# Spreading expert gates through one-hots: pairs of tokens instead of fours, the low part on one engine, evictions in another order

## The chip, the cores and the metric

The kernel is written in Bass with the Tile framework for Trainium2 and runs on one core of one chip. The metric is the device time of one execution in microseconds (us). The time before is the median of three executions. A difference below 0.2% (about 6 us) is taken as no change.

## The reference

A two-layer encoder of 512 tokens and width 1024. Each layer is attention (a global and a windowed group of heads) with a layer norm, and then a retrieval layer over 16384 experts of one neuron each:

```
for every token and each of 8 heads:
  s1, i1 = the 16 best of 128 first sub-keys;  s2, i2 = the 16 best of 128 second sub-keys
  the 16 best of the 256 sums s1 + s2 -> gates g = softmax, expert = i1 * 128 + i2
  a = gelu(u[expert] . x);   out += g * a * v[expert]
h = layer_norm(alpha * h + out)
```

So every token has 128 slots (8 heads by 16), each with a gate and two indices from 0 to 127.

## The kernel before, in words

Chunk 0 of 128 tokens (`gat`) gathers the rows of its experts. The other three chunks (`dense`, 384 tokens) are computed against all experts, in 128 blocks of 128, as plain matrix products with the gate of (expert, token) as a factor, zero nearly everywhere. That factor must first be built as a dense array `G`, laid out as [group of 32 tokens][128 first indices][128 second indices][32 tokens] and kept in DRAM. Building it is the stage of this study, the **spread** (`spread()`, once per layer). It has 48 iterations of eight tokens; four iterations make one group of 32 tokens and fill one staging tile `stg`.

The 128 slots of a token lie on the partitions. In an iteration VectorE compares the numbers 0 to 127 with the tokens' indices (L817) and gets the one-hots `o12`: `o1` of the first index and `o2` of the second, in fp16. The gates come as a sum of two fp16 parts: `a_h` is `o1` times the high part (L818, VectorE), `a_l` is `o1` times the low part. `a_l` is made half by VectorE (four tokens in one instruction, L819) and half by ScalarE (four tokens in four instructions, L821). Then TensorE multiplies for each token `o2` (stationary) by `a_h` and adds `o2` by `a_l` (L826, L827): 16 matmuls of 128x128 in an iteration, four tokens to a PSUM bank. ScalarE moves each of the two banks into `stg` (L829). When a group is full, SyncE's queue writes `stg` to `G` (L835), in two pieces.

In memory the one-hots of four tokens are interleaved: tokens are the innermost index, four fp16 values (8 bytes) wide, so a matmul on one token reads its 128 values 8 bytes apart. `o12`, `a_h` and `a_l` have two buffers each, `acc` banks in PSUM there are six, `stg` two (one in each of two pools).

Between the iterations run the first of the expert products, `acts()`: the dense tokens times one block of expert rows `ut` in full fp32 (L770, eight matmuls of 128x384, each of which the trace shows as two records) and a gelu by ScalarE (L781). One such block is asked for in every fourth iteration. After the spread come the experts (L777 to L779 and L961 to L963 on TensorE). The Tile framework orders each engine's instructions itself from the program and then each engine runs its own list in order; queue, buffers and semaphores do the rest. SyncE issues the DMAs in its own list, with a ring of four buffers (`wst`) for all large weights.

Of the kernel before, what the change touches and what calls it, by code (L numbers as in the profile page):

```python
# [45 lines left out]
def encoder_kernel(ctx: ExitStack, tc: tile.TileContext, x, ln_in_g, ln_in_b, w_in, qn_g, kn_g, sink,  # L46
# [27 lines left out]
    def bc(ap, shape):  # L74
        return ap.to_broadcast(shape)
# [6 lines left out]
    def rsqrt(src, scale, eps, n, nm):  # L82
        """y = (src * scale + eps) ** -0.5 for a [P, n] operand"""
        a = sm.tile([P, 16], F32, tag="rs_a", name=nm + "a")[:, :n]
        y = sm.tile([P, 16], F32, tag="rs_y", name=nm + "y", bufs=4)[:, :n]
        t = sm.tile([P, 16], F32, tag="rs_t", name=nm + "t")[:, :n]
        v.tensor_scalar(a, src, float(scale), float(eps), op0=MUL, op1=ADD)
        v.tensor_scalar(y.bitcast(I32), a.bitcast(I32), -0.5, 1597463007.0, op0=MUL, op1=ADD)
        for _ in range(3):
            v.scalar_tensor_tensor(t, y, -0.5, y, op0=MUL, op1=MUL)  # L90
            v.tensor_tensor(out=t, in0=t, in1=a, op=MUL)  # L91
            v.scalar_tensor_tensor(y, t, 1.5, y, op0=ADD, op1=MUL)  # L92
        return y
# [6 lines left out]
    def moments(st):  # L100
        """mean and 1 / deviation from the statistics of two halves"""
        mv = sm.tile([P, 2], F32, tag="ln_mv", name="ln_mv")
        v.bn_aggr(out=mv, in_=st.rearrange("p a b -> p (a b)"))
        return mv[:, 0:1], rsqrt(mv[:, 1:2], 1.0, LN_EPS, 1, "lnr")
# [17 lines left out]
    def transpose_rows(src, dst, nm, lo=None, gain=None, halves=(0, 1)):  # L122
        """src [P, 1024] -> dst [P, 8, P] with dst[:, k, :] = src[:, k-th 128].T"""
        for q in halves:
            qs = slice(q * 4, (q + 1) * 4)
            b = acc_bank(nm)
            for i in range(4):
                k = q * 4 + i
                pe.transpose(b[:, i * P:(i + 1) * P], src[:, k * P:(k + 1) * P], ident)
            bv = b.rearrange("p (k t) -> p k t", k=4)  # L130
            if gain is not None:
                v.tensor_tensor(out=dst[:, qs, :], in0=bv, in1=bc(gain[:, qs, None], [P, 4, P]), op=MUL)
            else:
                act.copy(dst[:, qs, :], bv)
            if lo is not None:
                v.tensor_tensor(out=lo[:, qs, :], in0=bv, in1=dst[:, qs, :].bitcast(F32), op=SUB)
# [12 lines left out]
    nc.sync.dma_start(ident, ident_c)  # L149
    iota4 = cp.tile([P, P, 4], F16, name="iota4")  # L150
    nc.sync.dma_start(iota4.rearrange("p n t -> p (n t)"), iota4_c)
    look = cp.tile([P, 3, TK, 8], F16, name="look")
# [7 lines left out]
    for l in range(L):  # L160
# [3 lines left out]

# [1 line left out]
        gq = bload(qn_g[l], HD, "gq")  # L166
# [14 lines left out]
        def norm_rope(src, n, c, dst):  # L181
            """src, dst [P, n, 64]: rms norm over 64 and rotary, gains in the tables"""
            nr = pj.tile([P, 3, 8, HD], F32, tag="nr", name="nr", bufs=1)
# [22 lines left out]
        def load_split(src, nm):  # L206
            """a [1024, 256] weight as halves of 512 rows, each an exact sum of two f32r parts"""
            w = load_w(src, nm)
# [69 lines left out]

# [1 line left out]
        pj.release()  # L280
# [5 lines left out]
        def begin(c, part):  # L286
            """queries of four heads: the two f32r parts below each other, transposed"""
            if part == 0:
# [123 lines left out]

# [1 line left out]
        Q = dr.tile([P, PH, 2, P], F32, tag="Q", name=f"Q{l}")  # L414

        def sub_keys(cs, xT):
            """the best 16 sub-keys of both query halves of all heads, in steps"""
            n = len(cs) * P
# [7 lines left out]
            def split(w, p_):  # L426
                """the weights of one query half as two f32r parts"""
                wp = w[:, :, p_ * P:(p_ + 1) * P]
# [60 lines left out]
        def top16(rows):  # L489
            """the 16 largest of each row and their places, for (values, places, row) of several rows in turn"""  # L490
            for i in range(2):
# [13 lines left out]
        def fold(t, dst):  # L505
            """sum over axis 1 of t [P, 16, J] into dst [P, J]"""
            for n in (8, 4, 2):
# [12 lines left out]
        def pair_steps(st, c, tl):  # L520
            """the 16 best pairs of each head: gates and both key indices"""
            sv, ix = st["sv"], st["ix"]
# [21 lines left out]
            v.tensor_copy(xf.rearrange("p a h k -> p (a h k)"), ix.rearrange("p a h k -> p (a h k)"))  # L544
            # differences of the first index list: i1[a] is the sum of the first a + 1 of them
            v.tensor_copy(df[:, :, 0:1], xf[:, 0, :, 0:1])
# [171 lines left out]
        def gates(c):  # L718
            """gates, as two fp16 parts, and key indices with the slots on the partitions"""
            b = acc_bank("ps_t")  # L720
# [6 lines left out]
            gh = ga.tile([P, P], F16, tag="gh", name="gh", bufs=3)  # L727
            glf = ga.tile([P, P], F32, tag="glf", name="glf", bufs=3)
            gl = ga.tile([P, P], F16, tag="gl", name="gl", bufs=3)
# [5 lines left out]
            act.copy(iT.rearrange("p o a t -> p a o t"), b[:, P:3 * P].rearrange("p (a o t) -> p a o t", a=2, t=8))  # L735
            flat[c] = gh, glf, gl, iT

# [8 lines left out]
        sp = sbuf(f"sp{l}", bufs=2, side="right")  # L746
        sp.tile([P, 4, P, 4], F16, tag="o12", name="o12")
        for tag in ("ah", "al"):
            sp.tile([P, 2, P, 4], F16, tag=tag, name=tag)
        xTd = xd.tile([P, KD, ND], F32, name="xTd")  # L750
# [9 lines left out]
        def acts():  # L760
            """gelu of the dense tokens on one block of 128 experts after another"""
            for g2 in range(NB // 2):
# [21 lines left out]

# [1 line left out]
        vts = []  # L786
# [13 lines left out]
        def spread():  # L800
            for c in dense:
                for tg in range(P // TG):
                    stg = (sp, lp)[tg % 2].tile([P, NB, TG], F32, tag="stg", name="stg", bufs=1)
                    for t8 in range(TG // 8):
                        gh, glf, gl, iT = flat[c]
                        o = tg * TG + t8 * 8
                        shp = [P, 2, P, 4]

                        def tv(ap):
                            return bc(ap[:, o:o + 8].rearrange("p (q t) -> p q t", t=4)[:, :, None, :], shp)  # L810
                        sh2 = [P, 4, P, 4]
                        o12 = sp.tile(sh2, F16, tag="o12", name="o12")
                        o1, o2 = o12[:, 0:2], o12[:, 2:4]
                        iu = iT[:, o // 8].rearrange("p a (q t) -> p (a q) t", t=4)
                        a_h = sp.tile(shp, F16, tag="ah", name="ah")
                        a_l = sp.tile(shp, F16, tag="al", name="al")
                        v.tensor_tensor(out=o12, in0=bc(iota4[:, None, :, :], sh2), in1=bc(iu[:, :, None, :], sh2), op=EQ)  # L817
                        v.tensor_tensor(out=a_h, in0=o1, in1=tv(gh), op=MUL)  # L818
                        v.tensor_tensor(out=a_l[:, 1], in0=o1[:, 1], in1=bc(gl[:, None, o + 4:o + 8], [P, P, 4]), op=MUL)  # L819
                        for t in range(4):  # L820
                            act.activation(a_l[:, 0, :, t], o1[:, 0, :, t], AF.Copy, scale=glf[:, o + t:o + t + 1])  # L821
                        for q in range(2):
                            b = acc_bank("ps_g")
                            for t in range(4):
                                bs = b[:, t * P:(t + 1) * P]
                                pe.matmul(bs, o2[:, q, :, t], a_h[:, q, :, t], start=True, stop=False)  # L826
                                pe.matmul(bs, o2[:, q, :, t], a_l[:, q, :, t], start=False, stop=True)  # L827
                            t0 = t8 * 8 + q * 4
                            act.copy(stg[:, :, t0:t0 + 4].rearrange("p n t -> p t n"),  # L829
                                     b.rearrange("p (t n) -> p t n", t=4))  # L830
                        yield
# [23 lines left out]

# [1 line left out]
        ga.release()  # L857
# [181 lines left out]
def _layout(inputs):  # L1039
# [5 lines left out]
    def blocks(w, n):  # L1045
        """[L, 1024, n*256] -> [L, n, 128, 8*256]"""
        return w.reshape(L, KD, P, n, 256).transpose(0, 3, 2, 1, 4).reshape(L, n, P, KD * 256)
# [47 lines left out]
```

## Time and profile before

| | |
|---|---|
| three executions | 3176.3, 3172.87, 3172.13 us (median 3172.87) |
| the profiled execution: time, span of its trace | 3176.3 us, 3176.1 us |
| instructions | 47802 |
| TensorE busy | 97% of the span, weight loads 88% |
| VectorE, ScalarE, GpSimd busy | 77%, 45%, 24% |
[...]

The spread takes about 155 us in each layer, from 429 to 585 us in layer 0 and from 2000 to 2156 us in layer 1. Matmul durations in the trace are modelled and overlap; the distance from one start to the next says more than the duration. A row with a count (x4) stands for several instructions in a row: its second number reaches from the first start to the last end.

### The profile page before, as it was taken

To read this page: it belongs to the slowest core of one execution; us is meant where nothing else is said; L and a number is where in the kernel's file an instruction comes from. 1 tells how busy PE (TensorE), PEld (TensorE's weight loads), DVE (VectorE), ACT (ScalarE), POOL (GpSimd) and SP (SyncE) were. 2 spreads that over 40 slices of the span, in tenths; PEclk is the share of its full clock that TensorE was granted. 3 is DMA by queue.
4 is the path that set the end of the run, shared out by engine and by line. 5 is a ranking of instruction groups with operands and counts; after the bars stand their busy time and mean duration, and the time that the engine had idled before them with its cause. 6 is when DMAs were issued, how large, how long until landed. Compare 5 with 4: busy or idle time off the path is not lost. (4 is left out here: it accounts for less than half of the span.)

```text
span 3176.1 us, 47802 instructions
## 1 busy us (share of the span) xinstructions
PE 3078.8 (97%) x17858; PEld 2793.2 (88%) x17858; DVE 2443.1 (77%) x5206; ACT 1440.9 (45%) x2778; POOL 759.3 (24%) x524
## 2 busy tenths in 40 slices
PE   6999899999999999999999999999999999999998
PEld 6989888799999999999888888888999999999997
DVE  6777976677777777777777779766687777877777
ACT  2664279643333333333337542994433333333332
POOL 0000000005444445445000000000054433544540
PEclk9999999999999999999999999999999999999999
DMA  4113655648888888888520137556488888898882
GB/s 173 41 54 130 226 203 209 225 143 321 327 307 327 315 322 319 315 322 308 202 94 14 69 143 257 193 199 229 176 329 325 318 313 317 309 327 321 305 313 100
DMA packets 262233, 749.46 MB, mean 236 GB/s; under 512 B 19952, under 2 KB 130288, under 8 KB 231792
## 3 DMA queue, kind: packets, MB, share of 16 engines
q1 hardware_dynamic: 188272, 477.94, 41.6%
q0 software_dynamic: 73728, 268.47, 23.2%
q8 instruction: 140, 2.29, 0.3%
q14 instruction: 93, 0.76, 0.1%
HBM read 691.81 MB, written 54.53 MB: 235 GB/s over the span
## 5 line engine op out<-in xcount | busy, mean ns | idle before, releaser
L918 POOL DMA_INDIRECT gt<-in_dram,idx x512 | 753.1, 1471 | 2140.8 <-DVE idx L909 1286.6
L777 PE MATMUL ps_a<-xTh,uh 128*128 128x384 f32 x1824 | 609.9, 334 | 3.7 <-ACT uh L774 3.7
L779 PE MATMUL ps_a<-xTh,ul 128*128 128x384 f32 x1824 | 611.6, 335 | 0.0
L778 PE MATMUL ps_a<-xTl,uh 128*128 128x384 f32 x1824 | 610.2, 335 | 0.0
L963 PE MATMUL ff<-vh,wl 128*128 128x512 f32 x1476 | 576.0, 390 | 0.0
L961 PE MATMUL ff<-vh,wh 128*128 128x512 f32 x1476 | 574.4, 389 | 0.0
L962 PE MATMUL ff<-vl,wh 128*128 128x512 f32 x1476 | 574.0, 389 | 0.0
L994 ACT CAST vh<-vt 128x1024 fp32r<-128x1024 f32 x246 | 258.4, 1051 | 606.6 <-PE ff L963 308.9
L995 DVE TENSOR_TENSOR vl<-vt,vh 128x1024 fp32r<-128x1024 f32 x246 | 301.0, 1224 | 200.1 <-ACT vh L994 195.9
L777 PEld LDWEIGHTS ps_a<-xTh,uh 128*128 128x128 f32 x1824 | 342.4, 188 | 14.4 <-ACT uh L774 5.6
L778 PEld LDWEIGHTS ps_a<-xTl,uh 128*128 128x128 f32 x1824 | 342.4, 188 | 10.4
L1001 ACT CAST wh<-w 128x384 fp32r<-128x384 f32 x246 | 126.3, 513 | 484.0 <-DVE w L998 480.0
L924 DVE CUSTOM_DVE_ANT_0 junk<-gt,h 128x1024 bf16<-128x1024 f32 x256 | 313.0, 1223 | 41.2 <-DMA gt<-in_dram,idx 36.6
L779 PEld LDWEIGHTS ps_a<-xTh,ul 128*128 128x128 f32 x1824 | 342.2, 188 | 0.1
L963 PEld LDWEIGHTS ff<-vh,wl 128*128 128x128 f32 x1476 | 277.0, 188 | 57.7
L935 DVE SCALAR_TENSOR_TENSOR gacc<-gt,gw,gacc 128x1024 f32<-128x1024 f32 x252 | 311.3, 1279 | 18.4 <-DMA gt<-in_dram,idx 18.3
L961 PEld LDWEIGHTS ff<-vh,wh 128*128 128x128 f32 x1476 | 276.9, 188 | 49.6 <-ACT wh L1001 0.9
L962 PEld LDWEIGHTS ff<-vl,wh 128*128 128x128 f32 x1476 | 277.0, 188 | 48.8
L775 DVE TENSOR_TENSOR ul<-ut,uh 128x1024 fp32r<-128x1024 f32 x228 | 277.7, 1218 | 29.2 <-ACT uh L774 29.2
L774 ACT CAST uh<-ut 128x1024 fp32r<-128x1024 f32 x228 | 239.8, 1052 | 117.6 <-PE ps_a L778 115.6
L1002 DVE TENSOR_TENSOR wl<-w,wh 128x384 fp32r<-128x384 f32 x246 | 137.4, 559 | 155.5 <-ACT wh L1001 155.5
L817 DVE TENSOR_TENSOR o<-iota,iT 128x2048 f16<-128x2048 f16 x96 | 117.4, 1225 | 97.1 <-ACT al L821 62.0
(260 smaller groups left out, 5248.0 us busy)
## 6 DMA issues: line engine op xcount, KB each, us to landing
ut<-in_dram SPq DMA_DIRECT2D x128, 1024.0 KB
vt<-in_dram SPq DMA_DIRECT2D x128, 1024.0 KB
w_pq<-in_dram SPq DMA_DIRECT2D x48, 1024.0 KB
gg<-G SPq DMA_DIRECT2D x62, 768.0 KB
G<-stg SPq DMA_DIRECT2D x24, 1920.0 KB
w_o<-in_dram SPq DMA_DIRECT2D x24, 1024.0 KB
w_q<-in_dram SPq DMA_DIRECT2D x8, 1024.0 KB
gt<-in_dram,idx POOLq DMA_INDIRECT x512
```

The source lines that it names most:

```text
L775: v.tensor_tensor(out=ul.rearrange(ff), in0=us, in1=uh.rearrange(ff).bitcast(F32), op=SUB)
L777: pe.matmul(b[:, :ND], uh[:, k, :], xTh[:, k, :], start=k == 0, stop=False)
L778: pe.matmul(b[:, :ND], uh[:, k, :], xTl[:, k, :], start=False, stop=False)
L779: pe.matmul(b[:, :ND], ul[:, k, :], xTh[:, k, :], start=False, stop=k == KD - 1)
L918: pool.indirect_dma_start(out=t, out_offset=None, in_=src, in_offset=bass.IndirectOffsetOnAxis(ap=idx[:, j:j + 1], axis=0))
L924: v.tensor_tensor_reduce(out=jk, in0=t, in1=h[:, c, :], op0=MUL, op1=ADD, scale=1.0, scalar=0.0, accum_out=a_[:, j:j + 1])
L935: v.scalar_tensor_tensor(acc[j % 2], t, w_[:, j:j + 1], acc[j % 2], op0=MUL, op1=ADD)
L961: pe.matmul(b, wh[:, cs], vh[:, ns], start=blk == 0, stop=False)
L962: pe.matmul(b, wh[:, cs], vl[:, ns], start=False, stop=False)
L963: pe.matmul(b, wl[:, cs], vh[:, ns], start=False, stop=blk == NB - 1)
L994: act.copy(vh, vt[:, bi, :])
L995: v.tensor_tensor(out=vl, in0=vt[:, bi, :], in1=vh.bitcast(F32), op=SUB)
```

## The change

Four edits, all in the spread. The tokens are interleaved by two instead of four, so that a matmul's 128 values lie 4 bytes apart (`iota2` is cut out of the numbers 0 to 127 that the program loads, and the loaded table now sits in a buffer of the weight ring). `a_l` is one VectorE instruction for all eight tokens; ScalarE's four instructions are gone, and the fp32 low part `glf` that they read has one buffer instead of three. The evictions walk the bank in another order: before, the four tokens' 128 values one token after the other, which reads PSUM without gaps and writes `stg` 128 bytes apart; now, for each value the four tokens, which reads PSUM 512 bytes apart and writes runs of four (16 bytes). Comments are taken out as well.

```diff
-    iota4 = cp.tile([P, P, 4], F16, name="iota4")
-    nc.sync.dma_start(iota4.rearrange("p n t -> p (n t)"), iota4_c)
+    iota4 = ws.tile([P, 2048], F32, tag="wst", name="iota4").bitcast(F16)[:, :P * 4]
+    nc.sync.dma_start(iota4, iota4_c)
+    iota2 = cp.tile([P, P, 2], F16, name="iota2")
+    v.tensor_copy(iota2, iota4.rearrange("p (n t) -> p n t", t=4)[:, :, 0:2])
...
-            glf = ga.tile([P, P], F32, tag="glf", name="glf", bufs=3)
+            glf = ga.tile([P, P], F32, tag="glf", name="glf", bufs=1)
...
-                        shp = [P, 2, P, 4]
+                        shp = [P, 4, P, 2]
 
                         def tv(ap):
-                            return bc(ap[:, o:o + 8].rearrange("p (q t) -> p q t", t=4)[:, :, None, :], shp)
-                        sh2 = [P, 4, P, 4]
+                            return bc(ap[:, o:o + 8].rearrange("p (q t) -> p q t", t=2)[:, :, None, :], shp)
+                        sh2 = [P, 8, P, 2]
...
-                        iu = iT[:, o // 8].rearrange("p a (q t) -> p (a q) t", t=4)
+                        iu = iT[:, o // 8].rearrange("p a (q t) -> p (a q) t", t=2)
...
-                        v.tensor_tensor(out=o12, in0=bc(iota4[:, None, :, :], sh2), in1=bc(iu[:, :, None, :], sh2), op=EQ)
+                        v.tensor_tensor(out=o12, in0=bc(iota2[:, None, :, :], sh2), in1=bc(iu[:, :, None, :], sh2), op=EQ)
                         v.tensor_tensor(out=a_h, in0=o1, in1=tv(gh), op=MUL)
-                        v.tensor_tensor(out=a_l[:, 1], in0=o1[:, 1], in1=bc(gl[:, None, o + 4:o + 8], [P, P, 4]), op=MUL)
-                        for t in range(4):
-                            act.activation(a_l[:, 0, :, t], o1[:, 0, :, t], AF.Copy, scale=glf[:, o + t:o + t + 1])
+                        v.tensor_tensor(out=a_l, in0=o1, in1=tv(gl), op=MUL)
                         for q in range(2):
                             b = acc_bank("ps_g")
                             for t in range(4):
                                 bs = b[:, t * P:(t + 1) * P]
-                                pe.matmul(bs, o2[:, q, :, t], a_h[:, q, :, t], start=True, stop=False)
-                                pe.matmul(bs, o2[:, q, :, t], a_l[:, q, :, t], start=False, stop=True)
+                                r, e = q * 2 + t // 2, t % 2
+                                pe.matmul(bs, o2[:, r, :, e], a_h[:, r, :, e], start=True, stop=False)
+                                pe.matmul(bs, o2[:, r, :, e], a_l[:, r, :, e], start=False, stop=True)
                             t0 = t8 * 8 + q * 4
-                            act.copy(stg[:, :, t0:t0 + 4].rearrange("p n t -> p t n"),
-                                     b.rearrange("p (t n) -> p t n", t=4))
+                            act.copy(stg[:, :, t0:t0 + 4], b.rearrange("p (t n) -> p n t", t=4))
```

The order on ScalarE in the spread of layer 0, four iterations of before (`al` is the low part, `stg` an eviction, `ge` the gelu of a block):

```order
L829 COPY stg<-ps_g 128x4x128 x4
L821 ACTIVATE al<-o_5305,glf 128x128 x4
L821 ACTIVATE al<-o_5335,glf 128x128
L781 ACTIVATE ge<-ps_a 128x384
L821 ACTIVATE al<-o_5335,glf 128x128 x3
L829 COPY stg<-ps_g 128x4x128 x4
L821 ACTIVATE al<-o_5365,glf 128x128 x4
L821 ACTIVATE al<-o_5398,glf 128x128 x4
```

and the same place of the change:

```order
L830 COPY stg<-ps_g 128x128x4 x8
L783 ACTIVATE ge<-ps_a 128x384
L830 COPY stg<-ps_g 128x128x4 x8
L783 ACTIVATE ge<-ps_a 128x384
L830 COPY stg<-ps_g 128x128x4 x8
```

Between two gelus stand eight evictions and nothing else.

TensorE in the same place, where one burst of matmuls of before ends and four matmuls of `acts()` follow in one piece, as they do behind every two iterations:

```order
L827 LDWEIGHTS o_5264
L827 MATMUL ps_g<-al,o_5264 128x128
L770 MATMUL ps_a<-xTd,ut 128x384 x4
L826 LDWEIGHTS o_5305
L826 MATMUL ps_g<-ah,o_5305 128x128
L827 LDWEIGHTS o_5305
L827 MATMUL ps_g<-al,o_5305 128x128
```

and the change, between the iterations with `o_5313` and `o_5339`:

```order
L828 MATMUL ps_g<-al,o_5313 128x128
L772 MATMUL ps_a<-xTd,ut 128x384
L827 LDWEIGHTS o_5339
L827 MATMUL ps_g<-ah,o_5339 128x128
L827 LDWEIGHTS o_5339
L827 MATMUL ps_g<-ah,o_5339 128x128
L772 MATMUL ps_a<-xTd,ut 128x384
L828 LDWEIGHTS o_5339
```

The matmuls of `acts()` now stand singly for most of the stage, one of them behind the first two products with `a_h`, in front of the first with `a_l`; per four iterations they are still eight.

SyncE at the end of the spread, before (`gg` is the first read of `G` for the experts, `vt` a load of expert rows):

```order
L795 DMA gg_5123<-G_5126 128x11x128
L835 DMA G_5126<-stg 128x256
L791 DMA vt<-in_dram 128x2x1024
L795 DMA gg_5123<-G_5126 128x128
L835 DMA G_5126<-stg 128x3840
```

and the change:

```order
L797 DMA gg_5125<-G_5128 128x11x128
L793 DMA vt<-in_dram 128x2x1024
L835 DMA G_5128<-stg 128x256
L797 DMA gg_5125<-G_5128 128x128
L835 DMA G_5128<-stg 128x3840
```

The load of `vt` has moved ahead of the small write of `G`; otherwise SyncE's list is the same, as is GpSimd's.

## Rows read from the trace of the kernel before

**Rows 1.** The page's first two parts: busy time of each engine with its share of the span and its number of instructions, and the busy share, in tenths, of TensorE (PE) and ScalarE (ACT) in 40 slices of 79 us.

```profile
PE 3078.8 (97%) x17858; PEld 2793.2 (88%) x17858; DVE 2443.1 (77%) x5206; ACT 1440.9 (45%) x2778; POOL 759.3 (24%) x524
...
PE   6999899999999999999999999999999999999998
...
ACT  2664279643333333333337542994433333333332
```

**Rows 2.** [...]

```profile
436.30:582.20 145.90, 145.90 (x920) 118.36 (x919) 99.80 (x136) 145.87 (x283) 0.00 (x0) 1.00 0.51 196
600.00:1140.00 540.00, 540.00 (x2748) 493.72 (x2747) 420.39 (x755) 202.73 (x270) 186.00 (x136) 1.00 0.79 288
2007.00:2152.00 145.00, 145.00 (x917) 118.00 (x916) 99.55 (x136) 144.97 (x282) 0.00 (x0) 1.00 0.51 196
```

**Rows 3.** Two groups of instructions by line and form in the spread of layer 0 (436.3 to 582.2 us); columns are the busy us of the group, mean ns of one, idle time of the engine before them and who ended it.

```profile
L817 DVE TENSOR_TENSOR o<-iota,iT 128x2048 f16<-128x2048 f16 x45 | 55.1, 1225 | 45.4 <-ACT al L821 31.0 <-PE ps_g L827 13.3 <-ACT stg L829 0.7
L827 PEld LDWEIGHTS <-o 128*128 128x128 f16 x369 | 42.9, 116 | 5.7 <-issue 5.0
```

**Rows 4.** TensorE in order of time, two rounds of two iterations in layer 0 (start us, duration us, what); 443.31 to 446.97 are 32 matmuls, the first, the second and the last of them shown.

```profile
443.31 0.28 PE L826 MATMUL ps_g<-ah,o 128*128 128x128 f16 x1
443.41 0.30 PE L827 MATMUL ps_g<-al,o 128*128 128x128 f16 x1
...
446.97 0.29 PE L827 MATMUL ps_g<-al,o 128*128 128x128 f16 x1
447.09 2.76 PE L770 MATMUL ps_a<-xTd,ut 128*128 128x384 f32 x8
449.68 0.28 PE L826 MATMUL ps_g<-ah,o 128*128 128x128 f16 x1
...
456.06 0.28 PE L826 MATMUL ps_g<-ah,o 128*128 128x128 f16 x1
```

**Rows 5.** ScalarE in order of time, one round of four iterations in layer 0 (start us, us from the first start to the last end, what, how many).

```profile
444.49 3.93 ACT L829 COPY stg<-ps_g 128x512 f32<-128x512 f32 x4
448.22 1.78 ACT L821 ACTIVATE al<-o,glf 128x128 f16<-128x128 f16 x5
449.74 0.59 ACT L781 ACTIVATE ge<-ps_a 128x384 f32<-128x384 f32 x1
450.22 1.18 ACT L821 ACTIVATE al<-o,glf 128x128 f16<-128x128 f16 x3
...
457.30 3.98 ACT L829 COPY stg<-ps_g 128x512 f32<-128x512 f32 x4
```

**Rows 6.** VectorE in order of time, one round of two iterations in layer 0, with its waits in brackets.

```profile
447.36 1.22 DVE L817 TENSOR_TENSOR o<-iota,iT 128x2048 f16<-128x2048 f16 x1 [0.67 <-PE ps_g L827]
448.50 0.69 DVE L818 TENSOR_TENSOR ah<-o,gh 128x1024 f16<-128x1024 f16 x1
449.10 0.42 DVE L819 TENSOR_TENSOR al<-o,gl 128x512 f16<-128x512 f16 x1
449.44 0.69 DVE L818 TENSOR_TENSOR ah<-o,gh 128x1024 f16<-128x1024 f16 x1
...
453.73 1.23 DVE L817 TENSOR_TENSOR o<-iota,iT 128x2048 f16<-128x2048 f16 x1 [0.67 <-PE ps_g L827]
```

**Rows 7.** TensorE in order of time, other matmuls, whose operands lie without gaps: 128x256 in a one-pass 4-byte type (the first and the last of 22), 24 transposes of 128 columns in a row, and 128x512 in the one-pass type (the first and the last of nine).

```profile
331.09 0.28 PE L474 MATMUL ps_pq<-xT,wql 128*128 128x256 f32 x1
...
333.61 0.28 PE L474 MATMUL ps_pq<-xT,wql 128*128 128x256 f32 x1
...
426.63 2.78 PE L129 MATMUL tr_x<-ident,h 128*128 128x128 f32 x24
...
610.12 0.39 PE L961 MATMUL ff<-vh,wh 128*128 128x512 f32 x1
...
611.93 0.39 PE L963 MATMUL ff<-vh,wl 128*128 128x512 f32 x1
```

**Rows 8.** Six ScalarE copies of a whole bank whose source and target both lie without gaps, and two VectorE operations on 4-byte elements one behind the other.

```profile
427.52 3.04 ACT L134 COPY xTd<-tr_x 128x512 f32<-128x512 f32 x6
...
596.94 1.22 DVE L775 TENSOR_TENSOR ul<-ut,uh 128x1024 fp32r<-128x1024 f32 x1 [15.42 <-ACT uh L774]
598.08 1.22 DVE L995 TENSOR_TENSOR vl<-vt,vh 128x1024 fp32r<-128x1024 f32 x1
```

**Rows 9.** SyncE's queue at the end of the spread in layer 0, and the DMA rate in 40 slices of 3.65 us from 436.3 to 582.2 us.

```profile
586.78 0.32 SPq L835 DMA_DIRECT2D G<-stg  x1
...
588.55 0.32 SPq L795 DMA_DIRECT2D gg<-G  x1
...
GB/s 0 2 4 381 335 146 171 409 0 0 373 335 155 137 442 0 0 373 294 200 173 404 2 0 373 281 213 171 404 0 4 373 314 177 171 404 7 0 356 267
```

**Rows 10.** ScalarE and VectorE where the spread of layer 0 goes over into the experts.

```profile
584.81 1.94 ACT L829 COPY stg<-ps_g 128x512 f32<-128x512 f32 x2 [0.60 <-PE ps_g L827]
...
595.48 0.49 ACT L781 ACTIVATE ge<-ps_a 128x384 f32<-128x384 f32 x1 [4.67 <-PE ps_a L770]
...
599.21 0.55 DVE L998 SCALAR_TENSOR_TENSOR w<-gg,ge 128x384 f32<-128x384 f32 x1
```

**Rows 11.** Two rows of VectorE in the first 25 us of the program.

```profile
14.15 0.20 DVE L103 BATCH_NORM_AGGREGATE ln_mv<-ln_st 128x2 f32<-128x12 f32 x1
...
21.84 2.36 DVE L215 TENSOR_TENSOR wlo<-w_k,whi 128x1024 fp32r<-128x1024 f32 x2 [3.86 <-ACT whi L214]
```

More of the change, by code (lines that the diff above doesn't have):

```diff
@@ L735, in gates @@
             act.copy(iT.rearrange("p o a t -> p a o t"), b[:, P:3 * P].rearrange("p (a o t) -> p a o t", a=2, t=8))
-            flat[c] = gh, glf, gl, iT
+            flat[c] = gh, gl, iT
         for c in order[:2]:
@@ L746, in encoder_kernel @@
         sp = sbuf(f"sp{l}", bufs=2, side="right")
-        sp.tile([P, 4, P, 4], F16, tag="o12", name="o12")
+        sp.tile([P, 8, P, 2], F16, tag="o12", name="o12")
         for tag in ("ah", "al"):
-            sp.tile([P, 2, P, 4], F16, tag=tag, name=tag)
+            sp.tile([P, 4, P, 2], F16, tag=tag, name=tag)
         xTd = xd.tile([P, KD, ND], F32, name="xTd")
@@ L804, in spread @@
                     for t8 in range(TG // 8):
-                        gh, glf, gl, iT = flat[c]
+                        gh, gl, iT = flat[c]
                         o = tg * TG + t8 * 8
-                        shp = [P, 2, P, 4]
+                        shp = [P, 4, P, 2]
                         def tv(ap):
-                            return bc(ap[:, o:o + 8].rearrange("p (q t) -> p q t", t=4)[:, :, None, :], shp)
-                        sh2 = [P, 4, P, 4]
+                            return bc(ap[:, o:o + 8].rearrange("p (q t) -> p q t", t=2)[:, :, None, :], shp)
+                        sh2 = [P, 8, P, 2]
                         o12 = sp.tile(sh2, F16, tag="o12", name="o12")
-                        o1, o2 = o12[:, 0:2], o12[:, 2:4]
-                        iu = iT[:, o // 8].rearrange("p a (q t) -> p (a q) t", t=4)
+                        o1, o2 = o12[:, 0:4], o12[:, 4:8]
+                        iu = iT[:, o // 8].rearrange("p a (q t) -> p (a q) t", t=2)
                         a_h = sp.tile(shp, F16, tag="ah", name="ah")
                         a_l = sp.tile(shp, F16, tag="al", name="al")
-                        v.tensor_tensor(out=o12, in0=bc(iota4[:, None, :, :], sh2), in1=bc(iu[:, :, None, :], sh2), op=EQ)
+                        v.tensor_tensor(out=o12, in0=bc(iota2[:, None, :, :], sh2), in1=bc(iu[:, :, None, :], sh2), op=EQ)
                         v.tensor_tensor(out=a_h, in0=o1, in1=tv(gh), op=MUL)
-                        v.tensor_tensor(out=a_l[:, 1], in0=o1[:, 1], in1=bc(gl[:, None, o + 4:o + 8], [P, P, 4]), op=MUL)
-                        for t in range(4):
-                            act.activation(a_l[:, 0, :, t], o1[:, 0, :, t], AF.Copy, scale=glf[:, o + t:o + t + 1])
+                        v.tensor_tensor(out=a_l, in0=o1, in1=tv(gl), op=MUL)
                         for q in range(2):
```

## The prediction, made before the result was known

> **What bounds the kernel now.** I read the page first, then the busy time by stretch, then each engine in order of time in the stage that the diff touches. The page says that TensorE is busy in 97% of the span, with the weakest slices at the start and end [rows 1]; ScalarE is at 45% over the whole, but has two humps that reach nine tenths, and these are the two spreads. [...] A matmul's duration is modelled, so I check TensorE by its starts: 32 products of the one-hots start 0.1187 us apart (443.41 to 446.97 in 30 steps), then eight records of `acts()` take 2.59 us (447.09 to 449.68), and the next burst starts at once; a round of two iterations lasts 6.38 us and holds no gap [rows 4]. ScalarE is as full: an eviction comes every 0.93 us (3.73 for four), a scaled copy every 0.30, a gelu costs 0.48; 8 x 0.93 + 16 x 0.303 + 0.48 = 12.8 for four iterations, which is the distance from 444.49 to 457.30 and twice TensorE's 6.38 [rows 5]. Two engines stand at the limit together. VectorE waits, 31.0 us for ScalarE and 13.3 for TensorE before the compare of these 145.9 us [rows 3, 6].
>
> So the stage gets shorter only if *both* get faster, and then by no more than the next limit allows. The experts behind it are TensorE's alone and move as a whole.
>
> **ScalarE.** The 16 scaled copies go: 4.85 us of 12.8. The eight evictions stay and change their order. Now they read without gaps and write one value per 128 bytes: 0.93 us. Six copies of the same size without gaps on either side take 3.04 us in all, 0.5 each [rows 8]. A PSUM read with gaps is not in the trace. Bounds: 0.5, if only the write side costs, and 1.87, if the reads cost twice what the writes do now. I take 0.93, the nearest row, one gap for another: 8 x 0.93 + 0.48 = 7.9 us per four iterations, 3.96 per round. ScalarE stays off the path up to 1.2 us an eviction.
>
> **VectorE.** `a_l` grows from 512 to 1024 elements per partition. Start to start, the compare costs 1.14, `a_h` 0.60, `a_l` 0.34 [rows 6]; the new `a_l` is like `a_h`, 0.60. An iteration is 2.34, a round 4.68 of 6.38. The runs of equal step shrink from four fp16 to two. No row has runs of two. Bounds: the same 2.34, or the price per element of 4-byte operands, 1.14 us for 1024 [rows 8], twice what `a_h` pays: 2.28 + 1.14 + 1.14 = 4.56. I take 2.34, since a pair is still 4 bytes in a row in all three operands.
>
> **TensorE.** Sixteen matmuls per iteration as before, reading every 4 bytes instead of every 8. This is the term that decides. One-pass matmuls of 4-byte operands without gaps start 0.120 us apart for 256 columns (331.09 to 333.61 in 21 steps) and 0.226 for 512 (610.12 to 611.93 in 8): 0.415 ns a column and 13.5 ns fixed [rows 7]. For 128 columns that gives 0.067. The one-hot products need 0.1187 for 128 columns: 51 ns more, as if each column took 0.82 ns, twice. In address per time both are alike: 4 bytes in 0.415 ns, 8 bytes in 0.82, about 10 bytes per ns. If TensorE is held by how fast it moves through memory, 4 bytes apart gives 0.067 back. Upper bound: 0.1187, if the step was never the cause. Between them lie the transposes: 128 columns without gaps and still 0.109 apart ((2.78 - 0.27) / 23) [rows 7], which speaks for a price per weight load; but they are 4-byte data in another mode, and I cannot tell whether they stream at one column per cycle. I take 0.067: it is the only value in which three rows of ordinary matmuls fit one line.
>
> [...]
>
> **The round after.** TensorE 32 x 0.067 + 2.59 = 4.73; VectorE 4.68; ScalarE 3.96. TensorE and VectorE come out equal, and with two buffers each hands over to the other: a compare starts only when the products of two iterations ago are done. I add 0.3, half of the 0.67 that VectorE now waits for TensorE in a round [rows 6], since the matmuls of `acts()` stand singly in the new order and leave shorter holes: 5.05 us. Against 6.38 that is 1.33 per round; the 48 iterations are 23.5 rounds behind the first one: 31 us a layer, 62 in both.
>
> **What I count as nothing.** DMA: 196 GB/s over 145.9 us [rows 2], in bursts with gaps at zero [rows 9]; the same bytes in 145.9 x 5.05 / 6.38 = 115 us are 248 GB/s, below the bursts' 335 to 442. A group's 2.1 MB (32 tokens x 16384 experts x 4 bytes) take some 6 us at that; its `stg` is wanted again one group (10.1 us) after, so the write hides, and even with 1 MB of `ut` ahead of it (3 us) it is just in time. The load of `vt` ahead of the last small write holds back `gg` by up to 3 us; the first use of `gg` stands at 599.21, 10.7 us behind its issue at 588.55, while TensorE finishes the last blocks of `acts()` until 595.48 [rows 9, 10]; without that cover it would cost those 3 us. The pair table costs VectorE one small copy at 14.15 us, about 0.2; VectorE idles 3.86 us before 21.84 [rows 11], so also a late table of that size hides. The table takes a ring buffer that the fourth weight load wants after the copy, which is no later than that load's issue.
>
> **Sum.** The profiled execution took 3176.3 us, 3.4 above the median; 3176.3 - 62 = 3114.3, and for the median 3172.87 - 62 = 3111.
>
> **The rivals.**
> *Weight loads bound TensorE.* For it: the transposes, and loads as long as the distance. Against it: the 13.5 ns line of the others. At 0.1187 the round stays 6.38, since ScalarE's relief is worth nothing behind a full TensorE: 3173. If the loads allow 0.109, a round gains 32 x 0.0097 = 0.31, in all 47 x 0.31 = 15: 3158. Values between 0.067 and 0.109 lie between.
> *VectorE pays the price of 4-byte operands* (other side). A round would be 9.12 instead of 6.38 and VectorE the bound: 47 x 2.74 = 129, so 3302. It decides from 3.19 us per iteration. For it: no row has runs of two, and half the price per element may hang on longer ones. Against: each operand keeps its 4-byte pairs.
> *Evictions get dearer* (other side). At 1.87 us a round of ScalarE is 4 x 1.87 + 0.24 = 7.7: 47 x 1.34 = 63, so 3236. It decides from 1.53 us. For it: every read jumps 512 bytes. Against: the jump on the write side costs only 0.93 - 0.5.
> *The change does not shorten the stage, but adds waits*: VectorE's finer handover with a TensorE as slow as now; up to 0.3 per round, 47 x 0.3 = 14: 3187.
>
> **Chances.** TensorE at about 0.067 and the rest as summed: 0.50, with its own range 3094 (4.73 a round, 47 x 1.65 = 78) to 3137 (TensorE at 0.085, 5.61 a round). TensorE between, with a gain of 7 to 36 us: 0.12. Unchanged: 0.20. VectorE the bound 0.09, evictions 0.05, added waits 0.04. Below 0.2% of the time (6 us) a measurement cannot tell the kernels apart. So faster 0.62, same 0.20, slower 0.18. The range takes the first three, 3094 to 3180.
>
> **What would show it.** Right: in the profile after, one-hot products start about 0.067 us apart and the loads no longer lie back to back; the compare stays 1.22 us and both products 0.69; ScalarE idles in the spread; the distance from one gelu to the next is 10.1 us instead of 12.8, and the experts' rows are unchanged, some 31 and 62 us earlier. Wrong: starts still 0.11 to 0.12 apart (then no gain, whatever ScalarE does); a compare of 2.2 us (VectorE); evictions above 1.5 us; or `stg` waiting for DMA. If TensorE speeds up and the stage does not follow, I have mis-sized the handover between the two buffers.

## The result and the profile after

The changed kernel takes 3097.35 us (median of four executions, 3096.31 to 3098.3), the kernel before 3172.5 (four executions beside it): ratio 0.9756, 95% interval 0.9742 to 0.977, 75 us faster. Forecast were 3111 and a gain of 62, in a range from 3094 to 3180; the time lies near its lower end.

The page of the kernel after, busy time of each engine, and two stretches of layer 0, the spread and the experts (columns, here and in [rows 2]: the stretch, its length, busy us of PE, PEld (weight loads), DVE (VectorE), ACT, POOL with their instructions, granted clock as a share of full speed, DMA share, GB/s):

```profile
PE 2999.2 (97%) x17858; PEld 2699.4 (87%) x17858; DVE 2468.8 (80%) x5207; ACT 1248.0 (40%) x2394; POOL 741.0 (24%) x524
```

```profile
436.30:540.00 103.70, 102.94 (x853) 68.96 (x850) 102.50 (x128) 50.41 (x97) 0.00 (x0) 1.00 0.65 254
560.00:1100.00 540.00, 540.00 (x2746) 493.45 (x2745) 421.21 (x755) 202.81 (x269) 182.67 (x137) 1.00 0.80 290
```

Against the first two rows of [rows 2], the spread and the experts of layer 0, the experts are as before (540 of 540 us TensorE, ScalarE 203). In the spread ScalarE has fallen from full (145.87 of 145.90 us) to half (50.41 of 103.70), and the engine without a gap is now VectorE, 102.50 of 103.70, where it had two thirds (99.80 of 145.90). TensorE still looks full, but its ends are modelled; by its starts (start us, duration, what; one iteration's products, `acts()` in between) it isn't:

```profile
481.28 0.22 PE L828 MATMUL ps_g<-al,o 128*128 128x128 f16 x1
...
482.02 0.22 PE L828 MATMUL ps_g<-al,o 128*128 128x128 f16 x1
482.08 0.86 PE L772 MATMUL ps_a<-xTd,ut 128*128 128x384 f32 x2
...
483.74 0.22 PE L828 MATMUL ps_g<-al,o 128*128 128x128 f16 x1
```

Fourteen one-hot products start from 481.28 to 482.02, 0.057 us apart, where [rows 4] had 0.1187. Then come records of `acts()`, and the next row of products begins 2.46 us after the first: 16 x 0.057 + 4 x 0.324 = 2.2 are work. VectorE shows why (in order of time, without a wait in brackets on any row):

```profile
446.69 1.21 DVE L819 TENSOR_TENSOR o<-iota,iT 128x2048 f16<-128x2048 f16 x1
447.94 0.69 DVE L820 TENSOR_TENSOR ah<-o,gh 128x1024 f16<-128x1024 f16 x1
448.55 0.68 DVE L821 TENSOR_TENSOR al<-o,gl 128x1024 f16<-128x1024 f16 x1
449.15 1.22 DVE L819 TENSOR_TENSOR o<-iota,iT 128x2048 f16<-128x2048 f16 x1
```

Compare, high part, low part, and the next compare 449.15 - 446.69 = 2.46 us behind the first: 1.25 + 0.61 + 0.60. The durations are those of [rows 6] (1.22 and 0.69), runs of two cost nothing that shows. ScalarE waits for TensorE ahead of nearly every pair of evictions, and a pair takes 1.07 us; [rows 5] had 3.93 for four. One of the pairs:

```profile
452.62 1.07 ACT L830 COPY stg<-ps_g 128x512 f32<-128x512 f32 x2 [1.34 <-PE ps_g L828]
```

TensorE's largest wait in the stretch 436.3 to 540 us (engine and line, whom it waits for, us in total, times, longest):

```profile
PEld L827 <- DVE ah L820: 12.7, 23, 1.1
```

The weight load ahead of the first product of an iteration waits for `ah`; some of the 12.7 us lie beside matmuls that still run. In [rows 6] it was VectorE that waited for TensorE.

**Where the 75 us come from.** All 14 blocks of `acts()` have to be through before the experts begin, also those behind the last eviction. So the stage is best counted as TensorE's work from its first one-hot product to the last record of `acts()`. TensorE before, in order of time: the first product, and what stands behind the last one; and all records of `acts()` there (count, ns of one, first and last start):

```profile
429.25 0.28 PE L826 MATMUL ps_g<-ah,o 128*128 128x128 f16 x1
...
585.19 10.26 PE L770 MATMUL ps_a<-xTd,ut 128*128 128x384 f32 x26
```

```profile
L770 PE MATMUL ps_a<-xTd,ut x224: 483/486/847, 431.1 to 595.0; 128*128 128x384 f32 x112
```

The kernel after, TensorE's first product and its last records of `acts()`, and the gelu of the last block:

```profile
427.83 0.22 PE L827 MATMUL ps_g<-ah,o 128*128 128x128 f16 x1 [0.16 <-ACT iT L737]
...
547.85 6.02 PE L772 MATMUL ps_a<-xTd,ut 128*128 128x384 f32 x18
```

```profile
553.90 0.49 ACT L783 ACTIVATE ge<-ps_a 128x384 f32<-128x384 f32 x1 [2.92 <-PE ps_a L772]
```

Before: 429.25 to 585.19 + 10.26 = 595.45, 166.2 us, of which 768 x 0.1187 = 91.2 are products (48 x 16 of them) and 224 x 0.324 = 72.6 `acts()` (2.59 / 8 a record, [rows 4]): 2.4 idle. After: 427.83 to 547.85 + 6.02 = 553.87, 126.0 us, 768 x 0.0573 = 44.0 (0.0573 is the mean distance in the bursts of the stage) and the same 72.6: 9.4 idle. Products give 47.2 back; 7.0 of it are lost again in waits, 1.0 of them for ScalarE's copy of `xTd` at the start of the stage, the others beside a VectorE without a gap; and the stage begins 1.4 earlier: 41.6 in layer 0, which is the distance between the gelus of the last block, 595.48 [rows 10] and 553.90. The 1.4 can't be laid to the change: in the profiles of the nine experiments below the first product stands anywhere from 426.42 to 429.37, and why is open. In layer 1 the last gelu of the stage stands 81.57 us earlier than before, 40.0 more:

```profile
2164.54 0.49 ACT L781 ACTIVATE ge<-ps_a 128x384 f32<-128x384 f32 x1 [4.67 <-PE ps_a L770]
```

```profile
2082.97 0.49 ACT L783 ACTIVATE ge<-ps_a 128x384 f32<-128x384 f32 x1 [2.92 <-PE ps_a L772]
```

These 81.6 are those of the two profiled executions; before's was 3.8 above its median, after's 1.0 below, and 1.6 lie outside the spans (3176.3 - 3176.1 against 3096.31 - 3094.5): 75.2.

### The profile page after: what moved, and what is told of

Its sections match the earlier page's. It is cut to its first block, busy times and chain, and to the rows that moved or that the text cites. A ratio compares the mean times of both kernels' runs of the same rounds, so it can differ in the third digit from the quotient of the medians.

```text
span 3094.5 us, 47374 instructions
## 1 busy us (share of the span) xinstructions
PE 2999.2 (97%) x17858; PEld 2699.4 (87%) x17858; DVE 2468.8 (80%) x5207; ACT 1248.0 (40%) x2394; POOL 741.0 (24%) x524
## 5 line engine op out<-in xcount | busy, mean ns | idle before, releaser
L918 POOL DMA_INDIRECT gt<-in_dram,idx x512 | 734.5, 1435 | 2078.8 <-DVE idx L909 1206.1
L780 PEld LDWEIGHTS ps_a<-xTl,uh 128*128 128x128 f32 x1824 | 342.4, 188 | 10.4
L772 PE MATMUL ps_a<-xTd,ut 128*128 128x384 f32 x448 | 172.7, 501 | 1.7 <-ACT xTd L134 1.7
```

The costliest lines, as they stand in the source:

```text
L780: pe.matmul(b[:, :ND], uh[:, k, :], xTl[:, k, :], start=False, stop=False)
L918: pool.indirect_dma_start(out=t, out_offset=None, in_=src, in_offset=bass.IndirectOffsetOnAxis(ap=idx[:, j:j + 1], axis=0))
```

## The experiments

The theory: TensorE's rate in the products is set by the distance of the values that it reads, TensorE and ScalarE stood at the limit together, and VectorE is the limit now. The rivals: ScalarE's relief alone made the gain; TensorE's alone did; the order of the evictions is a part of it; the distance matters through the weight loads.

**Four tokens interleaved, the rest of the change kept.**

```diff
...
-                        shp = [P, 4, P, 2]
+                        shp = [P, 2, P, 4]
...
-                        sh2 = [P, 8, P, 2]
+                        sh2 = [P, 4, P, 4]
...
```

> The whole change, but with four tokens interleaved as before (a matmul reads its 128 values 8 bytes apart): a_l all on VectorE, ScalarE with evictions in runs of four only. Theory A (the step of TensorE's operands set the 0.1187 us per product): products again 0.118 to 0.119 us apart, a round of two iterations 6.38 us, ScalarE half idle, time 3163 to 3173 (a shorter tail at most). Rival B (ScalarE's relief is the gain, the step nothing): products near 0.06 apart, time 3097 to 3130.

Measured: 3172.48 us, ratio 0.9992 (0.9983 to 1.0001). TensorE in order of time, the first and the last of twelve products, and busy time in the stage:

```profile
464.11 0.30 PE L828 MATMUL ps_g<-al,o 128*128 128x128 f16 x1
...
465.41 0.29 PE L828 MATMUL ps_g<-al,o 128*128 128x128 f16 x1
```

```profile
436.00:546.00 110.00, 110.00 (x690) 86.51 (x689) 84.41 (x101) 44.14 (x77) 0.00 (x0) 1.00 0.49 192
```

They stand (465.41 - 464.11) / 11 = 0.118 apart, ScalarE is busy 44 of 110 us, and nothing is gained. ScalarE's relief is worth nothing behind a full TensorE.

**The interleave by two alone.** ScalarE keeps half of `a_l`, the evictions their old order.

```diff
...
-                        v.tensor_tensor(out=a_l, in0=o1, in1=tv(gl), op=MUL)
+                        v.tensor_tensor(out=a_l[:, 2:], in0=o1[:, 2:], in1=tv(gl)[:, 2:], op=MUL)
+                        for t in range(4):
+                            act.activation(a_l[:, t // 2, :, t % 2], o1[:, t // 2, :, t % 2], AF.Copy, scale=glf[:, o + t:o + t + 1])
...
-                            act.copy(stg[:, :, t0:t0 + 4], b.rearrange("p (t n) -> p n t", t=4))
+                            act.copy(stg[:, :, t0:t0 + 4].rearrange("p n t -> p t n"),
+                                     b.rearrange("p (t n) -> p t n", t=4))
```

> The interleave by two alone: half of a_l stays with ScalarE (four scaled copies per iteration), evictions in the order of before. Theory A (two engines stood at the limit together): products about 0.057 apart in their bursts, but ScalarE full with 8 x 0.93 + 16 x 0.30 + 0.48 = 12.7 us per four iterations, so the spread keeps its length: 3165 to 3175. Rival B (TensorE alone was the bound, ScalarE only followed it): 3100 to 3130.

Measured: 3162.64 us, ratio 0.9962 (0.9948 to 0.9975). Busy time in the stage, and ScalarE in order of time:

```profile
436.00:546.00 110.00, 98.45 (x713) 63.84 (x712) 78.97 (x110) 109.99 (x228) 0.00 (x0) 1.00 0.53 206
```

```profile
447.42 0.49 ACT L783 ACTIVATE ge<-ps_a 128x384 f32<-128x384 f32 x1
...
452.19 2.51 ACT L823 ACTIVATE al<-o,glf 128x128 f16<-128x128 f16 x8
454.52 3.79 ACT L832 COPY stg<-ps_g 128x512 f32<-128x512 f32 x4
...
459.50 0.53 ACT L783 ACTIVATE ge<-ps_a 128x384 f32<-128x384 f32 x1
```

ScalarE is busy 109.99 of 110 us and sets the pace; the products of a burst stand 0.057 apart, and gelu to gelu is 12.1 us where [rows 5] had 12.8. So both limits were real, but the time lies just outside what I expected: eight scaled copies take 2.51 us here (2.67 to 2.75 before) and four evictions 3.79 (3.93 to 4.02). That the evictions, which are the same instructions, get 4% shorter was not expected; they do so in the next experiment too (3.82), where VectorE makes all of `a_l`. The cause stays open.

**The change with the old evictions** (the second hunk above alone).

> The change with the evictions of before (PSUM read without gaps, writes 128 bytes apart). Theory A (VectorE with 2.46 us per iteration is the bound now): evictions 0.93 instead of 0.49, ScalarE 8 x 0.93 + 0.48 = 7.9 us per four iterations against VectorE's 9.8, so the time stays: 3096 to 3100, perhaps one to two us more at the ends of the stage. Rival B (the new order of the evictions is a part of the gain): 3105 to 3120.

Measured: 3098.76 us, ratio 0.9761 (0.9747 to 0.9774), against 0.9756 of the change. ScalarE is busy 91.39 of 110 us and still not the limit; VectorE has the same 108.70 as in the change:

```profile
436.00:546.00 110.00, 108.42 (x894) 72.78 (x893) 108.70 (x136) 91.39 (x103) 0.00 (x0) 1.00 0.67 259
```

With `a_l` on VectorE the order of the evictions is worth nothing that shows.

**Eight tokens interleaved** (`shp = [P, 1, P, 8]`).

> The change with eight tokens interleaved (a matmul reads its 128 values 16 bytes apart). Theory A (TensorE's operands come at a rate of addresses, about 10 bytes per ns, once the step is wide enough): products 0.21 to 0.23 apart, a round 32 x 0.22 + 2.6 = 9.6 us instead of 6.4, 47 rounds x 3.2 = 150 us above the kernel before: 3300 to 3350. Rival B (a step over some limit costs one fixed factor of two, whatever its size): 0.118 apart, 3165 to 3175.

Measured, one execution: 3439.28 us. TensorE, the first and the last of 32 products, eight records of `acts()`, and the last records of the stage; then stretches with the granted clock in the third column from the end:

```profile
436.91 0.40 PE L828 MATMUL ps_g<-ah,o 128*128 128x128 f16 x1
...
444.14 0.41 PE L829 MATMUL ps_g<-al,o 128*128 128x128 f16 x1
...
456.38 4.89 PE L773 MATMUL ps_a<-xTd,ut 128*128 128x384 f32 x8
...
719.92 7.68 PE L773 MATMUL ps_a<-xTd,ut 128*128 128x384 f32 x18
```

```profile
436.00:440.00 4.00, 4.00 (x18) 2.42 (x17) 0.96 (x1) 1.07 (x2) 0.00 (x0) 1.00 0.00 0
440.00:444.00 4.00, 4.00 (x19) 2.50 (x18) 1.22 (x1) 1.17 (x2) 0.00 (x0) 0.53 0.00 0
456.00:460.00 4.00, 4.00 (x9) 2.26 (x8) 3.40 (x5) 0.58 (x1) 0.00 (x0) 0.50 0.79 334
436.00:546.00 110.00, 110.00 (x367) 63.77 (x366) 45.08 (x55) 23.55 (x41) 0.00 (x0) 0.69 0.24 96
```

7.23 / 31 = 0.233 us: 0.057, 0.118 and 0.233 for 4, 8 and 16 bytes. The distance doubles with the step, and rival B falls; the time lies outside both ranges. The products alone cost 2 x 768 x (0.233 - 0.1187) = 176 us; the time is 264 above the kernel before. The rest is the clock, which no theory had moving. It stands at 1.00 where the stage of before runs, and here, with products 0.233 apart and no gap between TensorE's starts, at 0.69 in the mean of 110 us, and anywhere from 0.50 to 1.00 in stretches of 4 us. The products don't notice (the burst spans a stretch at 1.00 and one at 0.53, 18 and 19 records in 4 us), but the `acts()` between them do: at 0.50 eight records take 4.89 us, where [rows 4] had 2.76. The stage of layer 0 runs from its first product at 426.42 to 719.92 + 7.68 = 727.60, 301.2 us; 768 x 0.233 = 178.9 are products, and the 122.3 left are 49.7 more than the 72.6 of `acts()` before. With the 2.4 us that were idle before and a start 2.8 us earlier taken off, that is 44.5 in this layer; twice that, an estimate for layer 1, is 89 against the missing 88. The experts play next to no part: from 900 to 1500 us the clock is back at 1.00 (0.95 from 700 to 900 us, where the stage ends).

**Which operand.** The compare in two halves, with the stationary `o2` by fours and the moving `a_h`, `a_l` by twos, and the reverse.

```diff
+    iota4 = cp.tile([P, P, 4], F16, name="iota4")
...
-                        o1, o2 = o12[:, 0:4], o12[:, 4:8]
...
+                        o1 = o12[:, :8 * P].rearrange("p (q n t) -> p q n t", q=4, t=2)
+                        o2 = o12[:, 8 * P:].rearrange("p (q n t) -> p q n t", q=2, t=4)
...
-                        v.tensor_tensor(out=o12, in0=bc(iota2[:, None, :, :], sh2), in1=bc(iu[:, :, None, :], sh2), op=EQ)
+                        v.tensor_tensor(out=o1, in0=bc(iota2[:, None, :, :], [P, 4, P, 2]), in1=bc(iT[:, o // 8, 0].rearrange("p (q t) -> p q t", t=2)[:, :, None, :], [P, 4, P, 2]), op=EQ)
+                        v.tensor_tensor(out=o2, in0=bc(iota4[:, None, :, :], [P, 2, P, 4]), in1=bc(iT[:, o // 8, 1].rearrange("p (q t) -> p q t", t=4)[:, :, None, :], [P, 2, P, 4]), op=EQ)
...
```

> The change, but the stationary operand o2 interleaved by four tokens (its load reads 8 bytes apart), the moving operands a_h and a_l by two (4 bytes apart); the compare becomes two of half the size. Theory A (the step slows the moving stream only, and loads hide behind it): products 0.057 apart, the time that of the change plus at most 0.05 us per iteration for the split compare, 3097 to 3105. Theory B (each operand for itself is held by its bytes, and the longer of load and stream sets the distance): 0.118 apart, 3165 to 3175. Theory C (load and stream share one rate): 0.088 apart, a round of two iterations 32 x 0.088 + 2.6 = 5.4 us, 3115 to 3130.

> The reverse: the moving operands a_h and a_l interleaved by four (8 bytes apart), the stationary o2 by two (4 bytes apart); the compare in two halves. Theory A (moving stream only) and theory B (the longer of the two): products 0.118 apart, 3165 to 3175. Theory C (shared rate): 0.088 apart, 3115 to 3130. A fourth, D (only the load of the stationary operand is slowed): 0.057 here and 0.118 in the other one.

Measured: stationary by fours 3097.38 us, ratio 0.9752 (0.9737 to 0.9767), the same as the change; moving by fours 3169.34, ratio 0.998 (0.997 to 0.9989), nearly the kernel before. Of the first, sixteen products (the first and the last) and the weight loads (count, busy us, mean ns); of the second, thirteen products and the weight loads:

```profile
463.58 0.22 PE L828 MATMUL ps_g<-ah,o 128*128 128x128 f16 x1
...
464.48 0.22 PE L829 MATMUL ps_g<-al,o 128*128 128x128 f16 x1
```

```profile
L828 PEld LDWEIGHTS <-o 128*128 128x128 f16 x342 | 37.5, 114 | 20.5 <-DVE ah L820 10.4 <-issue 7.1
```

```profile
463.83 0.30 PE L828 MATMUL ps_g<-ah,o 128*128 128x128 f16 x1
...
465.23 0.30 PE L829 MATMUL ps_g<-al,o 128*128 128x128 f16 x1
```

```profile
L829 PEld LDWEIGHTS <-o 128*128 128x128 f16 x261 | 29.7, 114 | 5.0 <-issue 2.5
```

0.90 / 15 = 0.060 and 1.40 / 12 = 0.117. The moving stream is what is slowed. Theory A holds, B, C and D fall. The loads take 114 ns instead of 97 in the change, and hide: one starts every 0.060. But they take 114 in the second run too, where the stationary operand is only 4 bytes apart, so the length of a load's record does not tell which operand is wide. VectorE's four halves take 0.60 each here, 2.41 an iteration, a little less than 2.46; the time doesn't follow, since 22 records of `acts()` stand behind the last product instead of 18.

**No interleave** (each operand contiguous for a token).

```diff
...
-                        shp = [P, 4, P, 2]
+                        shp = [P, 8, P, 1]
...
-                        sh2 = [P, 8, P, 2]
+                        sh2 = [P, 16, P, 1]
...
```

> The change with no interleave at all: each token's 128 values lie without gaps (2 bytes apart), and the tokens' indices and gates are repeated 128 times for VectorE. Theory A (0.057 is what TensorE needs for 128 columns, the step of 4 bytes costs nothing any more): products 0.055 to 0.058 apart in their bursts; theory B (still held by bytes): 0.03 to 0.05. For VectorE, theory C (it keeps its rate only while each operand brings two fp16 in a row): compare 2.3 and products of the gates 1.15 to 1.2, an iteration about 4.6, 3097 + 96 x 2.1 = 3300; theory D (a repeated value costs nothing): compare 1.22, the time 3097 to 3100.

Measured, one execution: 3276.98 us. TensorE, the first and the last of fourteen products, and VectorE:

```profile
474.49 0.22 PE L828 MATMUL ps_g<-al,o 128*128 128x128 f16 x1
...
475.22 0.22 PE L828 MATMUL ps_g<-al,o 128*128 128x128 f16 x1
```

```profile
469.89 2.28 DVE L819 TENSOR_TENSOR o<-iota,iT 128x2048 f16<-128x2048 f16 x1
472.09 1.22 DVE L820 TENSOR_TENSOR ah<-o,gh 128x1024 f16<-128x1024 f16 x1
473.23 1.21 DVE L821 TENSOR_TENSOR al<-o,gl 128x1024 f16<-128x1024 f16 x1
```

0.73 / 13 = 0.056: below 4 bytes TensorE gains next to nothing more. VectorE pays nearly twice: start to start 2.20 for the compare and 1.14 for each product, 4.47 an iteration (two iterations of the same trace last 8.94); that is the rival "VectorE pays the price of 4-byte operands", one step further on than the change goes. 96 x (4.47 - 2.46) = 193 give 3290; the time is 13 less. Here the last gelu of `acts()` in the stage stands at 525.75, long before the last eviction, and the experts' first matmul starts right behind the last product (643.79 behind 643.72), where the change has 7.5 us between them (547.85 to 555.38): in two layers 15.

From 540 us on, with `acts()` done and TensorE waiting for VectorE between bursts, the granted clock falls here too: 0.83 in the mean from 430 to 600 us, where 460 to 475 us show 1.00. A burst at 0.50 (the first and the last of thirteen products, and the clock, third from the end):

```profile
642.44 0.31 PE L827 MATMUL ps_g<-ah,o 128*128 128x128 f16 x1
...
643.72 0.31 PE L828 MATMUL ps_g<-al,o 128*128 128x128 f16 x1
```

```profile
642.40:643.70 1.30, 1.30 (x13) 1.30 (x13) 1.06 (x1) 0.38 (x1) 0.00 (x0) 0.50 0.00 0
```

1.28 / 12 = 0.107 at 0.50, where the same products take 0.056 at 1.00. So at 2 bytes the distance goes with TensorE's clock, and at 16 bytes, above, it does not (0.233 at 1.00 and at 0.53): what holds the wide step back is not that clock.

**Part of `a_l` back to ScalarE**: four of eight tokens (the first hunk of the second experiment, with the new evictions), or two.

> The change, with two of the eight tokens of a_l given back to ScalarE (two scaled copies per iteration). Theory A (VectorE bounds the stage with 2.46 us per iteration and ScalarE has 5 of 9.8 us to spare): VectorE 1.25 + 0.61 + 0.47 = 2.33 per iteration, ScalarE 8 x 0.49 + 8 x 0.30 + 0.48 = 6.8 per four, so 96 x 0.13 = 12 us less: 3084 to 3090. Rival B (a third engine in the chain costs in waits what VectorE saves): 3095 to 3102.

> The change, with four of the eight tokens of a_l given back to ScalarE, as in the kernel before, with the interleave by two and the new evictions. Theory A: VectorE 1.25 + 0.61 + 0.34 = 2.20 per iteration, TensorE (32 x 0.057 + 2.59) / 2 = 2.21, ScalarE (8 x 0.49 + 16 x 0.30 + 0.48) / 4 = 2.30, so the three nearly equal and up to 96 x 0.16 = 15 us less than the change: 3082 to 3097. Rival B (three full engines hand over with waits): 3097 to 3110.

Measured: two tokens 3089.01 us, ratio 0.9726 (0.9712 to 0.9739); four tokens 3085.57, ratio 0.9714 (0.9701 to 0.9727). Both beat the change (0.9742 to 0.977). With four: busy time in the stage, then TensorE at the first product of the stage, at the two ends of a round of two iterations, and at the end of the stage:

```profile
436.30:535.00 98.70, 98.58 (x876) 72.67 (x874) 94.03 (x133) 98.69 (x278) 0.00 (x0) 1.00 0.72 278
```

```profile
428.63 0.22 PE L829 MATMUL ps_g<-ah,o 128*128 128x128 f16 x1
...
471.63 0.22 PE L829 MATMUL ps_g<-ah,o 128*128 128x128 f16 x1
...
473.46 2.80 PE L772 MATMUL ps_a<-xTd,ut 128*128 128x384 f32 x8
476.10 0.22 PE L829 MATMUL ps_g<-ah,o 128*128 128x128 f16 x1
...
538.64 8.60 PE L772 MATMUL ps_a<-xTd,ut 128*128 128x384 f32 x26
```

A round is 476.10 - 471.63 = 4.47 us: 32 products in 1.83 and eight records of `acts()` in 2.64. TensorE has no hole left; from 428.63 to 538.64 + 8.60 = 547.24 are 118.6 us for 116.6 of work. VectorE drops to 94.03 of 98.70, ScalarE is at 98.69, and theory A holds in both. That VectorE was the limit of the change is thus shown from the other side. Against the change the stage ends 6.6 us earlier in a layer, and the times differ by 11.8.

The kernel with four tokens is the change without its second edit, and it differs from the interleave alone, 3162.64, by nothing but the order of the evictions. So that order is worth 77 us where ScalarE makes half of `a_l`, and nothing where VectorE makes all of it: the change relieves ScalarE twice, and one relief is enough. The one that was superfluous, `a_l`, filled VectorE.

## Why the prediction was right, and where its sizes were off

**What bounds the kernel: right.** TensorE and ScalarE together; the first experiment relieves ScalarE alone and gains nothing, the second TensorE alone and gains 12 of 75 us. What bounds it afterwards was only half right: the forecast had TensorE and VectorE equal, and the runs show VectorE alone.

**TensorE, 0.067: the right mechanism, the size 17% long.** Measured 0.0573. (My sign for it, loads that no longer lie back to back, was none: they are 97 ns long and start every 57, so they overlap.) The line through [rows 7] had a fixed 13.5 ns; at 128 columns it isn't there in full. This is the largest term: 768 x 0.0097 = 7.4 us in a layer. The prediction's thought that TensorE is held by how fast it moves through memory, at about 10 bytes per ns, holds at a little less from 4 to 16 bytes (512 bytes in 57, 1024 in 118, 2048 in 233 ns: 9.0, 8.7, 8.8), but only for the moving operand, which the prediction did not tell apart. The transposes at 0.109, which spoke for a price per load, are not explained by any run; a price per load they don't show, since the products came to 0.057 with a load ahead of each.

**ScalarE, 0.93 an eviction: wrong, and harmless.** Measured 0.49, the lower bound, the price of a copy without gaps [rows 8]. Reading PSUM 512 bytes apart costs nothing that shows, and runs of 16 bytes no more than a write without gaps (0.49 against 3.04 / 6 = 0.51). I took the row with a gap as the nearest, one gap for another; the two sides aren't alike. Off the path in the change, this price decides in the version with half of `a_l` on ScalarE.

**VectorE, 2.34: right in each instruction, 0.12 short in the sum.** The compare in [rows 6] was priced at 1.14, its distance to a next instruction that doesn't read it. In the change `a_h` follows at once and reads it: 1.25. That the reading is the cause is argued from the order and not tested. Where two compares stand in a row, as in the version with two tokens on ScalarE, it is 1.14 again (2.28 for two):

```profile
473.20 2.36 DVE L819 TENSOR_TENSOR o<-iota,iT 128x2048 f16<-128x2048 f16 x2
475.48 0.69 DVE L820 TENSOR_TENSOR ah<-o,gh 128x1024 f16<-128x1024 f16 x1
```

**The handover of 0.3 a round: right sum, wrong story.** I added it to two equal engines, each waiting for the other. In the rows above VectorE waits for nobody, and in the whole stage it waits 0.3 us for TensorE (13.3 in [rows 3]). TensorE waits, 7.0 us more than before in a layer, about the 24 x 0.3 = 7.2 forecast. So the forecast round of 5.05 comes near the measured 4.93, twice VectorE's 2.46, by luck in part: TensorE was put 0.31 too long (4.73 for 4.42), VectorE 0.25 too short (4.68 for 4.93), and the 0.3 of a mutual wait that does not occur stands where VectorE's own work does.

**The ends of the stage: not counted.** I multiplied rounds and took 23.5 of them; and 4.73 + 0.3 is 5.03, not 5.05, half a microsecond in a layer. The stage counted as a whole has 24 rounds' worth of products. 7.4 from the product's price, 1.4 from the start (cause open, as said), the half round (0.7) and the slip (0.5) are 10.0 of the 10.4 us by which layer 0 beat the forecast of 31.2.

**What was counted as nothing: right.** The write of `stg` holds nobody up at 254 GB/s (forecast 248), the first use of `gg`, at 557.64, comes without a wait ahead of it, and the experts are unchanged. A delay by the table's copy at the start doesn't show: the stage begins no later.

**The rivals.** Weight loads as the bound: excluded by the operand experiment, where loads as long as before's (114 and 116 ns) go with products 0.060 apart. VectorE at the price of 4-byte operands: real, but at one token, not two; the compare takes 1.22 us with pairs and 2.28 without, and no run shows why. I had given this rival 9 in 100. Dearer evictions: the reverse. Added waits: 7 us a layer, behind a gain of 47.

## What to carry to other kernels

Look at the step of the operand that streams through TensorE, not at that of the stationary one (here 0.117 us a product with the first at 8 bytes, 0.060 with the second): interleave as far as VectorE needs it for its rate (here pairs of fp16, a compare of 1.22 us against 2.28 without) and no further. Where two engines are full together, relieve each once and ask which third engine pays; a second relief of the same engine is only load for the third. And count a stage in which two streams share TensorE by its whole work from first to last instruction, not by rounds, or the tail is missed.

## What the runs showed of the hardware that was not expected

- Moving operand in fp16, 128 columns: 0.056 us at 2 bytes, 0.057 at 4, 0.118 at 8, 0.233 at 16. Stationary operand at 8 bytes and moving at 4: 0.060. The records of the weight loads are 97 ns long with both operands at 4 bytes, and 112 to 116 as soon as either is at 8.
- With products 0.233 us apart the granted clock fell to a mean of 0.69 over 110 us of the stage (before: 1.00), although TensorE had no gap between its starts; the products kept their distance, eight fp32 records between them took 4.89 us at 0.50 for 2.76 before. At 2 bytes the products did follow the clock: 0.056 at 1.00, 0.107 at 0.50.
- ScalarE's copy of a bank of 128x512 costs 0.49 us with a PSUM side that jumps 512 bytes and an SBUF side written in runs of 16, and 0.93 with an SBUF side that writes single values 128 bytes apart.
